# Row sums of a 64 MB tensor on one core: a two-part layout, sums of big tiles on one engine, an early main store, and loads issued ahead of the opening barrier

## The chip, the cores and the metric

The kernel runs on 1 core of one Trainium2 chip. The metric is device time in microseconds (us); lower is better. All runs named here are of state fast, and every profile shows a granted clock of 1.0. A profile covers one execution, and its span is about 1.8 us shorter than the device time of the same execution (162.6 against 164.42 for the profile of the kernel before).

Names used below: DVE is VectorE, ACT is ScalarE, POOL is GpSimd, SP is SyncE, which issues all DMAs here. "SPq" is SP's instruction sequencer. The "opening barrier" is the wait at the start of the program that holds each engine until the others are there too (in the trace SP waits for PE's sequencer). A load "lands" when all 16 counts of its semaphore have arrived in the trace.

## The reference

```python
batch, seq, dim = 32, 512, 1024
x = np.random.randn(batch, seq, dim).astype(np.float32)      # 67.1 MB
out = (np.sum(x, axis=-1) / float(dim)).astype(np.float32)   # 16,384 sums, 64 KB
```

One pass over 67.1 MB, and hardly any output. The 16,384 rows are spread over 128 partitions, so each partition has J = 128 rows of D = 1024 floats (4 KB each).

## The kernel before

Each partition owns 128 neighbouring rows, so in HBM the partitions of one load are 512 KB apart. Nine big loads (eight of 14 rows, one of 8) go through three buffers; then come loads of 4 and 2 rows, one row, and the last row in two pieces. DVE sums most rows of a tile in one reduce; ACT sums the others one at a time through its accumulator.

```python
xr = x.tensor.reshape((P, J, D)).ap()
out_v = out.tensor.reshape((P, J)).ap()
bulk = [14] * 7 + [14, 8]
split = {14: 6, 8: 4, 4: 2, 2: 1}            # rows summed on ACT
tail = [4, 2]
...
def sums(t, j, rows):
    d = rows - split[rows]
    for r in range(d, rows):
        act_sum(res[:, j + r : j + r + 1], t[:, r, :])
    nc.vector.reduce_sum(out=res[:, j : j + d], in_=t[:, :d, :], axis=AX)

for i, rows in enumerate(bulk):
    t = pool.tile([P, 14, D], F32, name="t")          # pool has 3 buffers
    tc.keep_in_program_order(nc.sync.dma_start(out=t[:, :rows, :], in_=xr[:, j : j + rows, :]))
    sums(t, j, rows)
    j += rows
...                                                   # tail tiles, one single row
c = 704
t = one.tile([P, D], F32, name="last")
tc.keep_in_program_order(nc.sync.dma_start(out=t[:, :c], in_=xr[:, j, :c]))
tc.keep_in_program_order(nc.sync.dma_start(out=t[:, c:], in_=xr[:, j, c:]))
act_sum(part[:, 2:3], t[:, :c])
nc.vector.reduce_sum(out=part[:, 3:4], in_=t[:, c:], axis=AX)
nc.vector.tensor_scalar(out=res[:, j : j + 1], in0=part[:, 3:4], scalar1=part[:, 2:3],
                        scalar2=scale, op0=ADD, op1=MULT)
tc.keep_in_program_order(nc.sync.dma_start(out=out_v, in_=res))   # one store of 64 KB
```

## Time and profile before

| | before |
|---|---|
| device time, median of 4 runs | 164.17 us (164.04 to 164.25) |
| share of the span in which the hardware DMA queue is busy, mean of 16 engines | 96.5% |
| busy DVE, ACT | 49%, 38% |
| first load issued, first tile landed | 0.73 us, 20.60 us |
| last load landed, store issued, store landed, end of span | 159.35, 160.22, 161.77, 162.65 us |

Lines of the page of the kernel before: span, busy time by engine, and the DMA queue (packets, MB, share of 16 engines' time).

```profile
span 162.6 us, 213 instructions
DVE 79.3 (49%) x16; ACT 61.1 (38%) x115; POOL 0.2 (0%) x4
q1 hardware_dynamic: 2160, 67.18, 96.5%
```

The DMA queue is the only thing that is nearly always busy. One packet of 57,344 bytes (14 rows of one partition) takes 2.116 us at the median of the trace, which is 27.1 GB/s on each of 16 engines, 434 GB/s together. 67.11 MB at that rate take 154.8 us. The rest of the span is head and tail.

Timeline of the kernel before (columns: start us, duration us, engine, line, operation, out<-in, and in brackets the idle time before it and what ended that).

```profile
0.72 1.28 ACT L50 ACT_TABLE_LOAD   x1 [0.72 <-PEq L108]
0.73 46.15 SPq L61 DMA_DIRECT2D t<-in_x_dram  x5
20.63 8.69 DVE L56 TENSOR_REDUCE res<-t 128x8 f32<-128x8192 f32 x1 [20.63 <-DMA t<-in_x_dram]
37.80 8.69 DVE L56 TENSOR_REDUCE res<-t 128x8 f32<-128x8192 f32 x1 [8.49 <-DMA t<-in_x_dram]
54.87 8.69 DVE L56 TENSOR_REDUCE res<-t 128x8 f32<-128x8192 f32 x1 [8.38 <-DMA t<-in_x_dram]
...
105.81 8.69 DVE L56 TENSOR_REDUCE res<-t 128x8 f32<-128x8192 f32 x1 [8.25 <-DMA t<-in_x_dram]
...
122.77 8.69 DVE L56 TENSOR_REDUCE res<-t 128x8 f32<-128x8192 f32 x1 [8.27 <-DMA t<-in_x_dram]
...
159.03 0.76 ACT L50 ACTIVATE junk<-last 128x704 f32<-128x704 f32 x1 [0.32 <-DMA last<-in_x_dram]
159.40 0.47 DVE L87 TENSOR_REDUCE part<-last 128x1 f32<-128x320 f32 x1
159.98 0.21 DVE L88 TENSOR_SCALAR res<-part 128x1 f32<-128x1 f32 x1
160.22 0.35 SPq L91 DMA_DIRECT2D out_dram<-res  x1
```

DVE starts the first sum 0.03 us after its tile lands and the others about as soon, so the starts of its sums tell the landings. After the first, every sum of a 14-row tile waits about 8 us for a DMA: the engines have time to spare. The first landings are 17.17 and 17.07 us apart, the later ones (105.81 to 122.77) 16.96. At the head, SP issues nothing until 0.73 us, when the opening barrier releases the engines. At the end there is a fixed sequence: last landing, two short DVE operations, store, closing barriers.

### The profile page before, as it was taken

What the parts mean: (1) busy time and instruction counts of PE and PEld (TensorE: products, weight loads), DVE (VectorE), ACT (ScalarE), POOL (GpSimd) and SP (SyncE); (2) the same over time, 40 slices, a digit from 0 to 9 for tenths busy, and PEclk for the clock granted to TensorE, in tenths of its full rate; (3) what the DMA queues carried; (4) which work ended last, traced back from release to release, by engine and by line L of the source; (5) the groups of instructions that cost most, each with busy time, mean ns of one, the idle gap of its engine ahead of it and who ended that gap; (6) DMA issues with size and microseconds to landing.
All of it is one profiled execution on the core that took longest, in us unless ns stands there. A gap on an engine that the chain in (4) does not pass through costs nothing.

```text
span 162.6 us, 213 instructions
## 1 busy us (share of the span) xinstructions
DVE 79.3 (49%) x16; ACT 61.1 (38%) x115; POOL 0.2 (0%) x4
## 2 busy tenths in 40 slices
DVE  0000099207940596039801990099108930697893
ACT  3000096006800490029201940095007700692882
POOL 0000000000000000000000000000000000000000
DMA  6999999989999999899999999999999999998990
GB/s 226 451 451 451 451 437 395 437 353 409 451 451 451 451 451 437 381 423 395 423 423 451 451 453 451 451 451 437 409 409 423 409 423 423 443 435 383 423 373 22
DMA packets 2161, 67.18 MB, mean 413 GB/s; under 512 B 240, under 2 KB 496, under 8 KB 752
## 3 DMA queue, kind: packets, MB, share of 16 engines
q1 hardware_dynamic: 2160, 67.18, 96.5%
q14 instruction: 1, 0.01, 0.0%
HBM read 67.11 MB, written 0.07 MB: 413 GB/s over the span
## 4 chain that ended last, share of the span: by engine, by line
DMA 74%; DVE 18%; another core or an unknown queue 5%; SPq 1%; issue 0%; DVEq 0%
DMA t<-in_x_dram 48%; DMA tail<-in_x_dram 25%; DVE res L56 17%; DVE part L75 0%; SPq L61 0%; SPq L66 0%; DVE part L87 0%; DVE res L79 0%; DVE res L88 0%; DVE res L76 0%; DVEq L88 0%; DVEq L76 0%; DVEq L79 0%
## 5 line engine op out<-in xcount | busy, mean ns | idle before, releaser
L56 DVE TENSOR_REDUCE res<-t 128x8 f32<-128x8192 f32 (+1 forms) x9 | 73.9, 8212 | 79.9 <-DMA t<-in_x_dram 79.9
L50 ACT ACTIVATE junk<-t 128x1024 f32<-128x1024 f32 x52 | 52.5, 1009 | 96.7 <-DMA t<-in_x_dram 96.7
L50 ACT ACTIVATION_READ_ACCUMULATOR junk<-t 128x1 f32 x52 | 9.7, 186 | 0.0
L56 DVE TENSOR_REDUCE res<-tail 128x2 f32<-128x2048 f32 (+1 forms) x2 | 3.5, 1753 | 0.7 <-DMA tail<-in_x_dram 0.7
L50 ACT ACTIVATE junk<-tail 128x1024 f32<-128x1024 f32 x3 | 3.1, 1022 | 0.9 <-DMA tail<-in_x_dram 0.9
L50 ACT ACT_TABLE_LOAD x1 | 1.3, 1283 | 0.7 <-PEq L108 0.7
L50 ACT ACTIVATE junk<-last 128x704 f32<-128x704 f32 x1 | 0.8, 761 | 0.3 <-DMA last<-in_x_dram 0.3
L75 DVE TENSOR_REDUCE part<-row 128x1 f32<-128x704 f32 x1 | 0.9, 880 | 0.0
L50 ACT ACTIVATION_READ_ACCUMULATOR junk<-tail 128x1 f32 x3 | 0.6, 186 | 0.0
L50 ACT ACTIVATE junk<-row 128x320 f32<-128x320 f32 x1 | 0.4, 441 | 0.1
L87 DVE TENSOR_REDUCE part<-last 128x1 f32<-128x320 f32 x1 | 0.5, 475 | 0.0
L79 DVE TENSOR_SCALAR res<-res 128x126 f32<-128x126 f32 x1 | 0.2, 228 | 0.1
L88 DVE TENSOR_SCALAR res<-part 128x1 f32<-128x1 f32 x1 | 0.2, 214 | 0.1
L76 DVE TENSOR_SCALAR res<-part 128x1 f32<-128x1 f32 x1 | 0.2, 214 | 0.1
L50 ACT ACTIVATION_READ_ACCUMULATOR junk<-last 128x1 f32 x1 | 0.2, 187 | 0.0
L50 ACT ACTIVATION_READ_ACCUMULATOR junk<-row 128x1 f32 x1 | 0.2, 186 | 0.0
L108 POOL MEMSET const-bfloat16-1.0<- 128x1 bf16 x1 | 0.1, 101 | 0.0
L108 POOL MEMSET const-uint8-127<- 128x1 uint8 x1 | 0.1, 101 | 0.0
L108 POOL MEMSET const-float32-0.0<- 128x1 f32 x1 | 0.1, 98 | 0.2 <-issue 0.2
L108 POOL MEMSET const-float32-1.0<- 128x1 f32 x1 | 0.1, 98 | 0.0
## 6 DMA issues: line engine op xcount, KB each, us to landing
t<-in_x_dram SPq DMA_DIRECT2D x8, 7168.0 KB, 42.1
t<-in_x_dram SPq DMA_DIRECT2D x1, 4096.0 KB, 34.8
tail<-in_x_dram SPq DMA_DIRECT2D x1, 2048.0 KB, 39.3
tail<-in_x_dram SPq DMA_DIRECT2D x1, 1024.0 KB, 41.4
row<-in_x_dram SPq DMA_DIRECT2D x1, 512.0 KB, 42.2
last<-in_x_dram SPq DMA_DIRECT2D x1, 352.0 KB, 42.6
last<-in_x_dram SPq DMA_DIRECT2D x1, 160.0 KB, 42.5
out_dram<-res SPq DMA_DIRECT2D x1, 64.0 KB, 1.5
```

The costliest lines, as they stand in the source:

```text
L50: nc.scalar.activation(junk[:, :n], src, COPY, accum_out=dst)
L56: nc.vector.reduce_sum(out=res[:, j : j + d], in_=t[:, :d, :], axis=AX)
L75: nc.vector.reduce_sum(out=part[:, 1:2], in_=t[:, :c], axis=AX)
L76: nc.vector.tensor_scalar(out=res[:, j : j + 1], in0=part[:, 1:2], scalar1=part[:, 0:1], scalar2=scale, op0=ADD, op1=MULT)
L79: nc.vector.tensor_scalar_mul(out=res[:, :j], in0=res[:, :j], scalar1=scale)
L87: nc.vector.reduce_sum(out=part[:, 3:4], in_=t[:, c:], axis=AX)
L88: nc.vector.tensor_scalar(out=res[:, j : j + 1], in0=part[:, 3:4], scalar1=part[:, 2:3], scalar2=scale, op0=ADD, op1=MULT)
L108: nc = _bacc.Bacc("TRN2", target_bir_lowering=False, num_devices=1)
```

## The change

The intent is to shorten head and tail. The first loads are moved ahead of the opening barrier; the main part of the result (120 of 128 columns) is stored while the last loads still run, so only 4 KB are left for the end; to make each store contiguous in HBM the rows are dealt out in two parts (120 rows per partition, then 8), which puts the partitions of the main part 480 KB apart instead of 512 KB; the first six big tiles are summed on DVE alone; the last row comes in three pieces. The diff cut to its core (the body of the helper and the loops are as described; `q` takes the sums of the last eight rows, `r` ACT's share of the seventh of them):

```diff
+def start_loads_at_once(nc):
+    # moves SP's first DMA copies that wait for nothing (three loads) in front of
+    # SP's drain in the first block, that is, ahead of the opening barrier
+    ...
+    nc.at_finalize(start_loads_at_once)
-    xr = x.tensor.reshape((P, J, D)).ap()
-    out_v = out.tensor.reshape((P, J)).ap()
+    L = 8
+    M = J - L
+    x_main = bass.AP(tensor=x.tensor, offset=0, ap=[[M * D, P], [D, M], [1, D]])
+    x_last = bass.AP(tensor=x.tensor, offset=P * M * D, ap=[[L * D, P], [D, L], [1, D]])
+    o_main = bass.AP(tensor=out.tensor, offset=0, ap=[[M, P], [1, M]])
+    o_last = bass.AP(tensor=out.tensor, offset=P * M, ap=[[L, P], [1, L]])
-    bulk = [14] * 7 + [14, 8]
-    split = {14: 6, 8: 4, 4: 2, 2: 1}
-    tail = [4, 2]
+    main = [(14, 0)] * 6 + [(14, 4), (14, 6), (8, 4)]      # (rows, of these on ACT)
+    last = [(4, 2), (2, 1)]
 ...
-    (last row: 704 columns on ACT, 320 on DVE, one tensor_scalar, one store of 64 KB)
+    a, b = 448, 704
+    load(pa, x_last[:, L - 1, :a])
+    load(pb, x_last[:, L - 1, a:b])
+    load(pc[:, : D - b], x_last[:, L - 1, b:])
+    nc.gpsimd.tensor_scalar_mul(out=res, in0=res, scalar1=scale)
+    tc.keep_in_program_order(nc.sync.dma_start(out=o_main, in_=res))      # behind the loads
+    act_sum(pc[:, D - b : D - b + 1], pa)
+    nc.vector.reduce_sum(out=pc[:, D - b + 1 :], in_=pb, axis=AX)
+    nc.vector.reduce_sum(out=q[:, L - 1 :], in_=pc, axis=AX)
+    nc.vector.scalar_tensor_tensor(out=fin, in0=q, scalar=scale, in1=r, op0=MULT, op1=ADD)
+    tc.keep_in_program_order(nc.sync.dma_start(out=o_last, in_=fin))
```

More of the change, by code (lines that the diff above doesn't have):

```diff
@@ L12 @@
 AX = mybir.AxisListType.X
+def start_loads_at_once(nc):
+    sp = mybir.EngineType.SP
+    first, body = nc.main_func.blocks[0], nc.main_func.blocks[1]
+    loads = []
+    for i in body.instructions:
+        if i.engine == sp:
+            if type(i).__name__ != "InstDMACopy" or (i.sync_info and i.sync_info.on_wait):
+                break
+            loads.append(i)
+    names = {i.name for i in loads}
+    assert names
+    body.instructions = [i for i in body.instructions if i.name not in names]
+    at = next(
+        k for k, i in enumerate(first.instructions) if i.engine == sp and type(i).__name__ == "InstDrain"
+    )
+    first.instructions = first.instructions[:at] + loads + first.instructions[at:]
 @with_exitstack
@@ L29 @@
     assert J * P == N
-    xr = x.tensor.reshape((P, J, D)).ap()
-    out_v = out.tensor.reshape((P, J)).ap()
-    bulk = [14] * 7 + [14, 8]
-    split = {14: 6, 8: 4, 4: 2, 2: 1}
-    tail = [4, 2]
-    assert sum(bulk) + sum(tail) + 2 == J
-    pool = ctx.enter_context(tc.tile_pool(name="bulk", bufs=3))
+    L = 8
+    M = J - L
+    x_main = bass.AP(tensor=x.tensor, offset=0, ap=[[M * D, P], [D, M], [1, D]])
+    x_last = bass.AP(tensor=x.tensor, offset=P * M * D, ap=[[L * D, P], [D, L], [1, D]])
@@ L41 @@
+    o_main = bass.AP(tensor=out.tensor, offset=0, ap=[[M, P], [1, M]])
+    o_last = bass.AP(tensor=out.tensor, offset=P * M, ap=[[L, P], [1, L]])
+    main = [(14, 0)] * 6 + [(14, 4), (14, 6), (8, 4)]
+    last = [(4, 2), (2, 1)]
+    assert sum(n for n, _ in main) == M and sum(n for n, _ in last) == L - 2
+    bulk = ctx.enter_context(tc.tile_pool(name="bulk", bufs=3))
     one = ctx.enter_context(tc.tile_pool(name="one", bufs=1))
     psum = ctx.enter_context(tc.tile_pool(name="junk", bufs=4, space=bass.MemoryType.PSUM))
-    res = one.tile([P, J], F32, name="res")
@@ L45, with load, act_sum @@
-    part = one.tile([P, 4], F32, name="part")
-    def act_sum(dst, src):
+    res = one.tile([P, M], F32, name="res")
+    fin = one.tile([P, L], F32, name="fin")
+    q = one.tile([P, L], F32, name="q")
+    r = one.tile([P, L], F32, name="r")
+    nc.gpsimd.memset(r, 0.0)
+    def load(dst, src):
+        tc.keep_in_program_order(nc.sync.dma_start(out=dst, in_=src))
+    def act_sum(dst, src, by=1.0):
         n = src.shape[-1]
         junk = psum.tile([P, D], F32, name="junk")
-        nc.scalar.activation(junk[:, :n], src, COPY, accum_out=dst)
@@ L52, in sums @@
-    def sums(t, j, rows):
-        d = rows - split[rows]
-        for r in range(d, rows):
-            act_sum(res[:, j + r : j + r + 1], t[:, r, :])
-        nc.vector.reduce_sum(out=res[:, j : j + d], in_=t[:, :d, :], axis=AX)
+        nc.scalar.activation(junk[:, :n], src, COPY, scale=by, accum_out=dst)
+    def sums(dst, t, rows, on_act):
+        d = rows - on_act
+        for i in range(d, rows):
+            act_sum(dst[:, i : i + 1], t[:, i, :])
+        nc.vector.reduce_sum(out=dst[:, :d], in_=t[:, :d, :], axis=AX)
@@ L58 @@
     j = 0
-    for i, rows in enumerate(bulk):
-        t = pool.tile([P, 14, D], F32, name="t")
-        tc.keep_in_program_order(nc.sync.dma_start(out=t[:, :rows, :], in_=xr[:, j : j + rows, :]))
-        sums(t, j, rows)
+    for rows, on_act in main:
+        t = bulk.tile([P, 14, D], F32, name="t")
+        load(t[:, :rows, :], x_main[:, j : j + rows, :])
+        sums(res[:, j : j + rows], t, rows, on_act)
         j += rows
-    for i, rows in enumerate(tail):
-        t = one.tile([P, rows, D], F32, name=f"tail{i}")
-        tc.keep_in_program_order(nc.sync.dma_start(out=t, in_=xr[:, j : j + rows, :]))
-        sums(t, j, rows)
-        j += rows
@@ L71 @@
-    c = 704
-    t = one.tile([P, D], F32, name="row")
-    tc.keep_in_program_order(nc.sync.dma_start(out=t, in_=xr[:, j, :]))
-    act_sum(part[:, 0:1], t[:, c:])
-    nc.vector.reduce_sum(out=part[:, 1:2], in_=t[:, :c], axis=AX)
-    nc.vector.tensor_scalar(
-        out=res[:, j : j + 1], in0=part[:, 1:2], scalar1=part[:, 0:1], scalar2=scale, op0=ADD, op1=MULT
-    )
-    nc.vector.tensor_scalar_mul(out=res[:, :j], in0=res[:, :j], scalar1=scale)
-    j += 1
-    t = one.tile([P, D], F32, name="last")
@@ L84 @@
-    tc.keep_in_program_order(nc.sync.dma_start(out=t[:, :c], in_=xr[:, j, :c]))
-    tc.keep_in_program_order(nc.sync.dma_start(out=t[:, c:], in_=xr[:, j, c:]))
-    act_sum(part[:, 2:3], t[:, :c])
-    nc.vector.reduce_sum(out=part[:, 3:4], in_=t[:, c:], axis=AX)
-    nc.vector.tensor_scalar(
-        out=res[:, j : j + 1], in0=part[:, 3:4], scalar1=part[:, 2:3], scalar2=scale, op0=ADD, op1=MULT
-    )
-    tc.keep_in_program_order(nc.sync.dma_start(out=out_v, in_=res))
+    j = 0
+    for rows, on_act in last:
+        t = one.tile([P, rows, D], F32, name=f"t{rows}")
+        load(t, x_last[:, j : j + rows, :])
+        sums(q[:, j : j + rows], t, rows, on_act)
+        j += rows
@@ new lines @@
+    c = 768
+    row = one.tile([P, D], F32, name="row")
+    load(row, x_last[:, j, :])
+    act_sum(r[:, j : j + 1], row[:, c:], by=scale)
+    nc.vector.reduce_sum(out=q[:, j : j + 1], in_=row[:, :c], axis=AX)
+    a, b = 448, 704
+    pa = one.tile([P, a], F32, name="pa")
+    pb = one.tile([P, b - a], F32, name="pb")
+    pc = one.tile([P, D - b + 2], F32, name="pc")
+    load(pa, x_last[:, L - 1, :a])
+    load(pb, x_last[:, L - 1, a:b])
+    load(pc[:, : D - b], x_last[:, L - 1, b:])
+    nc.gpsimd.tensor_scalar_mul(out=res, in0=res, scalar1=scale)
```

## The prediction

> **What bounds it now.** The load stream. By the page's queue part the hardware DMA queue is busy 96.5% of 16 engines' span, while DVE is busy 49% and ACT 38%. In the trace's packets, one of 57,344 bytes takes 2.116 us at the median: 27.1 GB/s on each of 16 engines, 434 GB/s together; 67.11 MB at that rate is 154.8 of the 162.6 us. In the timeline the 14-row tiles land 16.9 to 17.2 us apart. This is at the 435 GB/s ceiling that the Trainium skill gives ("DMA: Bandwidth & Descriptors", section Bandwidth); nothing in the change raises it.
>
> So only what lies outside the stream can move the time:
> - Head (queue's timeline): first load issued at 0.73 us, after the opening barrier; first packet at 1.74; the first packets are slow (2.5 to 3.0 us), about 0.6 us in all.
> - Tail: the last load lands at 159.35; DVE ends at 160.19, the store is issued at 160.22, its first packet starts at 161.07, it lands at 161.77, and the closing barriers end at 162.65.
>
> **What the change does.**
> 1. Loads ahead of the barrier: first issue from 0.73 to about 0.0. All 0.7 us is on the critical path. SP reaches the barrier after three issues (about 1.3 us), so ACT and DVE start later; they wait until 20 us for data, so that is free.
> 2. Big tiles on DVE alone: 8 rows take 8.69 us and 4 rows 4.42, so 1.07 us a row, about 15.1 us for 14, under the 17 us between landings. The buffer returns 15 us after landing instead of 8.7, with two loads queued behind it (about 19 us of work), so the stream doesn't starve. Nothing gained or lost: off the critical path.
> 3. Layout, 120 and 8 rows: the same bytes in the same large packets; the pitch between partitions becomes 480 KB instead of 512. The packets before show only some 0.75 us of slowness over the middle (mostly from 25 to 70 us), so this is worth between -0.5 and +0.3; I take -0.05. A third piece of the last row: eight more small packets per engine, +0.1 us with its landing.
> 4. Main store queued behind the loads: 61 KB leave the end; the scaling moves to POOL, done about 5 us before the end. The last store is 4 KB (32 bytes per partition). Only the 0.35 us of packet time shrinks, by perhaps 0.15; issue to first packet (0.85 us) and receipt (0.35 us) stay.
> 5. Last row: ACT does 448 columns, DVE 256, then DVE must reduce 322 after both, then multiply-add. From the last landing: the 256-column reduce ends 0.06 us after it, +0.12 wait, +0.48 reduce, +0.11 wait, +0.21: issue about 1.0 us after landing instead of 0.87, so +0.14.
>
> **Sum.** -0.73 (barrier) +0.1 (third piece) -0.05 (layout) +0.14 (DVE tail) -0.15 (store) = about -0.7 us. Predicted 163.55 us; 8 times in 10 between 163.0 and 164.2. Faster by over 2%: 1%; within 2%: 98%; slower by over 2%: 1%.
>
> **What would show it.** Queue's timeline: first issue near 0, first packet near 1.0, first tile landing near 19.9. Landings still 16.9 to 17.1 apart. DVE's 14-row sums near 15.1 us, idle about 1.9 us before each. The end: last landing near 158.7, final store issued about 1.0 us later and landing 1.3 to 1.5 us after that.
>
> **What would make it wrong.** The new pitch changing the packet time; the 32-byte writes landing slowly; the main store's packets colliding with the last loads or the last store; the device time not counting the 0.7 us of barrier; or DVE's 14-row sums taking over 17 us, which would starve the queue.

## The result, and the profile after

| | before | after |
|---|---|---|
| device time, median of 4 runs | 164.17 us (164.04 to 164.25) | 162.98 us (162.87 to 163.29) |

The ratio is 0.9931, 95% interval 0.9914 to 0.9948. The gain is 1.2 us by the medians where 0.7 was forecast. It is within 2%, as predicted, but the median lies 0.02 us below the low end of the stated range.

Page of the kernel after, the same lines as before:

```profile
span 161.5 us, 138 instructions
DVE 120.0 (74%) x15; ACT 20.7 (13%) x39; POOL 0.8 (0%) x6
q1 hardware_dynamic: 2448, 67.18, 97.1%
```

DVE took over ACT's work, and the queue is as busy as it was. Timeline of the kernel after:

```profile
0.00 52.27 SPq L76 DMA_DIRECT2D t<-in_x_dram  x5
1.73 1.28 ACT L81 ACT_TABLE_LOAD   x1 [1.73 <-PEq L144]
19.92 15.09 DVE L87 TENSOR_REDUCE res<-t 128x14 f32<-128x14336 f32 x1 [19.92 <-DMA t<-in_x_dram]
36.83 15.09 DVE L87 TENSOR_REDUCE res<-t 128x14 f32<-128x14336 f32 x1 [1.82 <-DMA t<-in_x_dram]
53.78 15.09 DVE L87 TENSOR_REDUCE res<-t 128x14 f32<-128x14336 f32 x1 [1.86 <-DMA t<-in_x_dram]
...
157.58 0.55 ACT L81 ACTIVATE junk<-pa 128x448 f32<-128x448 f32 x1
157.87 0.42 DVE L124 TENSOR_REDUCE pc<-pb 128x1 f32<-128x256 f32 x1
158.07 0.18 ACT L81 ACTIVATION_READ_ACCUMULATOR junk<-pa 128x1 f32 x1
158.38 0.49 DVE L125 TENSOR_REDUCE q<-pc 128x1 f32<-128x322 f32 x1
158.98 0.17 DVE L126 SCALAR_TENSOR_TENSOR fin<-q,r 128x8 f32<-128x8 f32 x1
159.17 0.34 SPq L127 DMA_DIRECT2D out_dram<-fin  x1
```

The first load is issued at 0.00 instead of 0.73. ACT's table load, released by the same barrier, starts 1.0 us later than before, and nothing waits for it. The first landings are 16.91 and 16.95 us apart, not 17.17 and 17.07. The last load lands at 158.25, so the store is issued 0.92 us after it, where the kernel before needed 0.88.

DMA issues of the two stores after, and of the one store before (KB each, us from issue to landing):

```profile
out_dram<-res SPq DMA_DIRECT2D x1, 60.0 KB, 5.1
out_dram<-fin SPq DMA_DIRECT2D x1, 4.0 KB, 1.4
```

```profile
out_dram<-res SPq DMA_DIRECT2D x1, 64.0 KB, 1.5
```

The main store is queued behind the last loads and lands 5.1 us after its issue; the small one lands 0.14 us sooner after its issue than the big one did (1.41 against 1.55 in the trace).

It helps to cut each span at three points: the first issue, the first landing, and the eighth landing (the last tile of 14 rows).

| stretch, us | before | after | difference |
|---|---|---|---|
| start of span to first issue | 0.73 | 0.00 | -0.73 |
| first issue to first landing | 19.87 | 19.90 | +0.03 |
| first to eighth landing | 119.07 | 118.58 | -0.49 |
| eighth landing to end of span | 22.97 | 23.04 | +0.07 |

The 0.73 was predicted, and so was the near zero of the last line. The 0.49 in the middle of the load stream was not. These are two single executions, however, and the profile of the kernel before fell on the slowest of its runs up to then (164.42).

### The profile page after: what moved, and what is told of

It reads as the page before. It is cut to its first block, busy times and chain, and to the rows that moved or that the text cites. A ratio compares the mean times of both kernels' runs of the same rounds, so it can differ in the third digit from the quotient of the medians.

```text
span 161.5 us, 138 instructions
## 1 busy us (share of the span) xinstructions
DVE 120.0 (74%) x15; ACT 20.7 (13%) x39; POOL 0.8 (0%) x6
## 4 chain that ended last, share of the span: by engine, by line
DMA 67%; DVE 29%; another core or an unknown queue 1%; SPq 1%; issue 0%; DVEq 0%
DMA t<-in_x_dram 45%; DVE res L87 28%; DMA row<-in_x_dram 22%; SPq L76 1%; DVE q L107 1%; DVE q L125 0%; DVE pc L124 0%; DVE fin L126 0%; DVEq L125 0%; DVEq L126 0%
## 5 line engine op out<-in xcount | busy, mean ns | idle before, releaser
L87 DVE TENSOR_REDUCE res<-t 128x14 f32<-128x14336 f32 (+3 forms) x9 | 114.4, 12716 | 38.2 <-DMA t<-in_x_dram 38.2
L81 ACT ACTIVATE junk<-t 128x1024 f32<-128x1024 f32 x17 | 17.2, 1013 | 135.6 <-DMA t<-in_x_dram 135.6
L87 DVE TENSOR_REDUCE q<-t 128x2 f32<-128x2048 f32 (+1 forms) x2 | 3.5, 1752 | 0.7 <-DMA t<-in_x_dram 0.7
L81 ACT ACTIVATION_READ_ACCUMULATOR junk<-t 128x1 f32 x17 | 3.2, 188 | 0.0
L120 POOL TENSOR_SCALAR res<-res 128x120 f32<-128x120 f32 x1 | 0.5, 513 | 151.0 <-DVE res L87 151.0
L107 DVE TENSOR_REDUCE q<-row 128x1 f32<-128x768 f32 x1 | 1.0, 953 | 0.1
L125 DVE TENSOR_REDUCE q<-pc 128x1 f32<-128x322 f32 x1 | 0.5, 489 | 0.1
L81 ACT ACTIVATE junk<-pa 128x448 f32<-128x448 f32 x1 | 0.5, 547 | 0.1
```

Of the source, the lines that this page charges most:

```text
L81: nc.scalar.activation(junk[:, :n], src, COPY, scale=by, accum_out=dst)
L87: nc.vector.reduce_sum(out=dst[:, :d], in_=t[:, :d, :], axis=AX)
L107: nc.vector.reduce_sum(out=q[:, j : j + 1], in_=row[:, :c], axis=AX)
L120: nc.gpsimd.tensor_scalar_mul(out=res, in0=res, scalar1=scale)
L125: nc.vector.reduce_sum(out=q[:, L - 1 :], in_=pc, axis=AX)
```

## The experiments

Kernels whose names start with b_ are the kernel before with one thing altered; those with a_ are the kernel after with one thing altered. Theory A: the middle got faster because of the load addresses (512 KB between partitions became 480). Theory B: it got faster because the engines use the buffers differently. Theory C: it is chance of single executions, and worth nothing on average.

### b_again: the kernel before, unchanged

> The kernel before, unchanged: a control for noise and a second trace of its middle. Both theories expect 164.17 us (ratio 1.000 within 0.001). In the first trace the eighth 14-row tile landed 119.07 us after the first, and the landings of tiles 2 to 4 were 17.18, 17.07 and 17.10 us apart against 16.91 to 16.95 later. Theory A (the address pattern, partitions 512 KB apart) expects the slow stretch again: 119.0 to 119.2 us. A third theory, chance of one execution, expects 118.6 to 119.3 us, with the slow stretch elsewhere or absent.

164.13 us (ratio 1.000, 0.9988 to 1.0012). The second trace has no slow stretch: 118.61 us from the first to the eighth landing. Load rate in the first three intervals between landings, first trace (columns: stretch, length, busy time of DVE, ACT, POOL, clock, DMA share, GB/s):

```profile
20.00:37.00 17.00, 8.69 (x1) 6.34 (x12) 0.00 (x0) 1.00 1.00 425
37.00:54.00 17.00, 8.69 (x1) 6.35 (x12) 0.00 (x0) 1.00 0.98 418
54.00:71.00 17.00, 8.69 (x1) 6.34 (x12) 0.00 (x0) 1.00 1.00 432
```

The same stretches of the second trace, b_again:

```profile
20.00:37.00 17.00, 8.69 (x1) 6.35 (x12) 0.00 (x0) 1.00 1.00 432
37.00:54.00 17.00, 8.69 (x1) 6.34 (x12) 0.00 (x0) 1.00 1.00 432
54.00:71.00 17.00, 8.69 (x1) 6.34 (x12) 0.00 (x0) 1.00 1.01 439
```

The same kernel with the same engine work moved 425 and 418 GB/s in one execution and 432 in the other. So the slow stretch comes and goes: the 0.49 us of the first comparison is not a fixed property, and Theory A in its strict form ("always") is wrong. The span of the second trace is 162.26 us, which is nearer to the usual run.

### b_barrier: only the loads moved ahead of the barrier

```diff
+    nc.at_finalize(start_loads_at_once)      # with the helper, nothing else
```

> The kernel before with only the loads moved ahead of the opening barrier. Both theories expect 0.7 us less than before (163.45 us, ratio 0.9957): first issue at 0.0, first tile landing at 19.9, and the middle (first to eighth landing) still 119.0 to 119.2 us. If the barrier alone were worth all that the change gained, it would be 162.98.

163.53 us, ratio 0.9963 (0.9951 to 0.9975): 0.6 us faster. The first issue is at 0.00 and the first landing at 19.83; the middle is 119.06 us. The head is as expected, and the time lies 0.1 us above the expected 163.45, which is within the noise. The barrier alone does not explain the whole gain.

### b_layout: only the load addresses

```diff
-in_=xr[:, j : j + rows, :]
+in_=x_main[:, j : j + rows, :]               # 480 KB apart; x_last for the last 8 rows
```

> The kernel before with only the load addresses changed: 120 rows per partition, 8 in a second part. The sums go to the old places, so the result is wrong on purpose (right sums, in a different order). Theory A (the middle of the stream was slow because of the address pattern) expects 118.6 us from the first to the eighth landing and 163.7 us in all (ratio 0.997). Theory B (the middle was slow because ACT and DVE both read the buffers during the loads, or because buffers return at another moment) expects no change: 119.07 us and 164.17.

163.86 us, ratio 0.9987 (0.9976 to 0.9999): 0.2 us faster, just clear of noise. Its output is wrong, which doesn't matter for the time. The middle took 118.69 us and the first landing came 19.73 us after the first issue.

### b_dve: only the split between DVE and ACT

```diff
-        d = rows - split[rows]
+        d = rows - (4 if j == 84 else 0 if rows == 14 and j < 84 else split[rows])
```

> The kernel before with only the split changed: tiles 1 to 6 on DVE alone, tile 7 with 4 rows on ACT, the rest as before. Theory A (address pattern) expects no change: 119.07 us from the first to the eighth landing, 164.17 us in all. Theory B (ACT's reads or the moment of the buffer's return slow the loads) expects 118.6 us and 163.7. DVE's 14-row sums 15.1 us in both.

164.20 us, ratio 1.0004 (0.9991 to 1.0017): nothing. Its trace shows a slow stretch again (118.97 us) although ACT is idle there. Theory B falls: ACT's reads are not what makes it.

### a_again: the changed kernel, unchanged

> The changed kernel, unchanged: a control and a second trace. The first batch showed that the slow stretch of the middle comes and goes between executions of the kernel before (119.07 and 118.61 us from first to eighth landing). Theory A' (the parts add up: barrier -0.7, layout -0.2, end of the kernel -0.05 to -0.1, average over executions) expects 163.0 to 163.2 us. Theory C (the gain of the first comparison held a lucky 0.4 us in the middle) expects 163.3 to 163.5.

162.97 us, ratio 0.9925 (0.9910 to 0.9940). The gain is confirmed at 1.2 us; Theory C (163.3 to 163.5) is wrong, and the time is just below the range of Theory A' (163.0 to 163.2). In this trace the middle is 118.59 us, no shorter than b_again's 118.61, yet its span is 161.07 against 162.26. Of these 1.19 us, 0.73 is the issue, 0.02 the middle, and 0.51 the stretch from first issue to first landing (19.44 us against 19.95), less 0.06 that the end takes longer. So there is a second place where the new kernel can gain: the first tile.

### a_pitch512: the changed kernel with the old addresses

```diff
-x_main = bass.AP(tensor=x.tensor, offset=0, ap=[[M * D, P], [D, M], [1, D]])
-x_last = bass.AP(tensor=x.tensor, offset=P * M * D, ap=[[L * D, P], [D, L], [1, D]])
+x_main = bass.AP(tensor=x.tensor, offset=0, ap=[[J * D, P], [D, M], [1, D]])
+x_last = bass.AP(tensor=x.tensor, offset=M * D, ap=[[J * D, P], [D, L], [1, D]])
 # and the stores likewise, so the result is right
```

> The changed kernel with the old addresses, partitions 512 KB apart in both parts (result right, stores strided). Theory A' (the layout matters on average, by rarer slow packets or a better start) expects +0.2 to +0.3 us over the changed kernel run in the same rounds. Theory C (the layout is worth nothing, the 0.2 us of the first batch was noise) expects 0.0, within 0.1.

163.58 us, ratio 0.9957 (0.9938 to 0.9977) against 0.9925 (0.9910 to 0.9940) for a_again in the same rounds: 0.5 us slower by the ratios, 0.6 by the medians, and more than either theory expected. The intervals just touch, but all six runs (163.12 to 163.83) lie above all five of a_again (162.85 to 163.07). It gives back over 40% of the gain of the whole change by addresses alone; order and kind of all instructions are those of the changed kernel. (The addresses of the stores change too; a_p512_onestore below, which stores as the kernel before does, is no faster than this one clear of noise.) The two traces differ by 0.40 us up to the first landing, 0.22 in the middle and 0.11 at the end. In the head one can see where the difference begins. These are windows of the first microseconds (a packet is counted where it starts, so 1835 GB/s over 0.5 us is 16 packets of 57,344 bytes, one on each engine). The kernel after:

```profile
1.00:1.50 0.50, 0.00 (x0) 0.00 (x0) 0.00 (x0) 1.00 6.06 1835
1.50:2.00 0.50, 0.00 (x0) 0.27 (x1) 0.10 (x1) 1.00 0.00 0
2.00:2.50 0.50, 0.00 (x0) 0.50 (x1) 0.00 (x0) 1.00 0.00 0
```

The same windows of a_pitch512:

```profile
1.00:1.50 0.50, 0.00 (x0) 0.00 (x0) 0.00 (x0) 1.00 3.47 1147
1.50:2.00 0.50, 0.00 (x0) 0.26 (x1) 0.10 (x1) 1.00 1.34 459
2.00:2.50 0.50, 0.00 (x0) 0.50 (x1) 0.00 (x0) 1.00 0.65 229
```

In the first of these traces (480 KB) all 16 engines start within half a microsecond. With 512 KB 10 start, then 4, then 2: the last one starts 2.02 us after the first issue.

But the packets that start together also take longer. The DMA share in these lines is the packets' own time over the window, as a share of 16 engines, so the 16 first packets take 3.03 us each on average with 480 KB (6.06 times 0.5) and 2.73 with 512 KB. In these two traces the last of them ends 4.77 and 4.69 us after the first issue, and the first tile lands after 19.90 and 19.84: in this execution the earlier start bought nothing. Over all 14 traces the first landing comes 15.10 to 15.19 us after the last of the 16 first packets has ended (by the packets of the trace; seven more of 2.116 us, 14.8 in all, follow on each engine). So what counts for the head is that end, and not the start of the sixteenth engine.

### a_act: the changed kernel with the old split

```diff
-    main = [(14, 0)] * 6 + [(14, 4), (14, 6), (8, 4)]
+    main = [(14, 6)] * 8 + [(8, 4)]
```

> The changed kernel with the old split, 6 of 14 rows on ACT in each big tile. Both theories expect no change against the changed kernel (within 0.1 us): the sums are off the critical path either way. A rival in which ACT's reads slow the loads expects +0.3 or more, with packets over 2.116 us spread over the middle.

163.11 us, ratio 0.9938 against 0.9925: 0.2 us slower than a_again, more than expected, but inside the intervals (0.9922 to 0.9954 and 0.9910 to 0.9940). Its trace has one landing interval of 17.11 us and is otherwise like a_again's. b_dve moved the other way (DVE alone was 0.07 us slower by its ratio). The two together show no effect of the split that is clear of noise; one of up to about 0.2 us is not excluded.

### a_p512_onestore: one store at the end

```diff
-    res = one.tile([P, M], F32, name="res")
-    fin = one.tile([P, L], F32, name="fin")
+    whole = one.tile([P, J], F32, name="whole")
+    res, fin = whole[:, :M], whole[:, M:]
-    ...dma_start(out=o_main, in_=res)
-    ...dma_start(out=o_last, in_=fin)
+    ...dma_start(out=out.tensor.reshape((P, J)).ap(), in_=whole)
```

> The changed kernel with the old addresses and one store of 64 KB at the very end, instead of 60 KB queued behind the loads and 4 KB at the end. To be compared with a_pitch512, which differs in the store alone. If the early store is worth what its landing times say (1.55 us from issue to landing before, 1.41 after), +0.15 us over a_pitch512, with 1.55 us again in the trace. If it is worth nothing, 0.0; if the receipts of 512-byte rows also delay the closing barrier, +0.3 or more.

The diff is cut, and against a_pitch512.

163.38 us, ratio 0.9953 (0.9938 to 0.9969) against 0.9957 for a_pitch512: no slower, where +0.15 was one of the three expectations. The intervals are too wide to exclude +0.15 by times alone. The trace does show 1.54 us from issue to landing instead of 1.41. But without the main store in the queue the last load landed 19.73 us after the eighth instead of 19.88, and the closing took 0.83 us after the store's landing instead of 0.93. From the eighth landing to the end it is 23.09 us against 23.14. With the early store the last store lands 0.13 us sooner after its issue, but the last load lands 0.15 later; 0.09 of that is hidden, because DVE was still busy with the middle piece (the store is issued 1.00 us after the last landing without it, 0.91 with it). The 0.10 at the close is the order in which SP waits for its semaphores (see a_oldtail below). Net, no gain of the early store shows.

### a_pitch508 and a_contig: other distances between partitions

```diff
# a_pitch508
-x_main = bass.AP(tensor=x.tensor, offset=0, ap=[[M * D, P], [D, M], [1, D]])
+x_main = bass.AP(tensor=x.tensor, offset=0, ap=[[127 * D, P], [D, M], [1, D]])
# a_contig: each tile one contiguous stretch, partitions 56 KB apart
-        load(t[:, :rows, :], x_main[:, j : j + rows, :])
+        part = bass.AP(tensor=x.tensor, offset=P * j * D, ap=[[rows * D, P], [D, rows], [1, D]])
+        load(t[:, :rows, :], part)
```

> The changed kernel, main part's partitions 508 KB apart instead of 480 (wrong result on purpose: 7 of 127 rows are skipped per partition). So far, with partitions 512 KB apart, the sixteenth queue's first packet started 2.0 us or more after the first issue and the first tile landed 19.83 to 19.98 us after it (six traces); with 480 KB, 1.35 to 1.6 us and 19.44 to 19.90 us (four traces). If it is the power of two that hurts, 508 KB behaves like 480: 1.6 us or less, 163.0 us. If it is closeness to 512 KB or the mere size of the pitch, it behaves like 512: 2.0 us, 163.5.

> The changed kernel, each tile of the main part one contiguous stretch of memory, partitions 56 KB apart (wrong result on purpose: right sums in another order). If the power of two is what hurts, this is like 480 KB: 163.0 us, within 0.15. If any smaller pitch is better, the start gets better still: under 1.35 us to the sixteenth queue's first packet and under 162.9 us in all.

Their outputs are wrong, which doesn't matter for the times. a_pitch508: 163.08 us, ratio 0.9930 (0.9914 to 0.9946); the sixteenth engine starts 1.36 us after the issue. a_contig: 163.03 us, ratio 0.9925 (0.9909 to 0.9940); 1.43 us. So 508 KB behaves like 480 KB and like 56 KB: being 4 KB off 512 is enough, and a smaller distance brings no more.

### a_oldtail: an attempt at a version that beats both

```diff
-    (last row in three pieces: 448 on ACT, 256 on DVE, 320 + 2 partial sums on DVE)
+    load(end[:, :704], x_last[:, L - 1, :704])
+    load(end[:, 704:], x_last[:, L - 1, 704:])
+    act_sum(part[:, 2:3], end[:, :704])
+    nc.vector.reduce_sum(out=part[:, 3:4], in_=end[:, 704:], axis=AX)
+    nc.vector.tensor_scalar(out=fin[:, L - 1 :], in0=part[:, 3:4], scalar1=part[:, 2:3],
+                            scalar2=scale, op0=ADD, op1=MULT)
```

> An attempt at a version that beats both: the changed kernel with the last row cut as in the kernel before (two pieces, 704 columns on ACT and 320 on DVE). From the eighth landing to the end the kernel before took 22.98 us and the changed one 23.03 to 23.05. If the third piece costs what the landings say, the last load lands 0.06 us earlier against the eighth (19.71), the store is issued 0.88 us after it instead of 0.92, and the stretch takes 22.9 us: about 0.1 us less than the changed kernel, 162.9 us.

The cut leaves out that the row before the last is also split as in the kernel before (704 columns on DVE), and that the first six of the last eight sums are scaled early.

162.77 us (162.68 to 162.88), ratio 0.9908 (0.9890 to 0.9926), result correct. It was not run in the same rounds as the changed kernel, and the intervals of the two ratios overlap (0.9925 for a_again), so by times alone "faster than the changed kernel" is likely but not proved. The trace gives the reason: from the eighth landing to the end 22.84 us against 23.03 to 23.04. The end of its timeline:

```profile
157.63 0.76 ACT L79 ACTIVATE junk<-last 128x704 f32<-128x704 f32 x1 [0.35 <-DMA last<-in_x_dram]
158.02 0.49 DVE L119 TENSOR_REDUCE part<-last 128x1 f32<-128x320 f32 x1
158.61 0.21 DVE L120 TENSOR_SCALAR fin<-part 128x1 f32<-128x1 f32 x1
158.85 0.34 SPq L123 DMA_DIRECT2D out_dram<-fin  x1
```

Its DVE starts the last reduce 0.03 us after the landing (157.99); in the changed kernel that reduce has to wait for the reduce of the middle piece and starts 0.13 us after it. The other part is at the close. SP waits there for the semaphores one after the other; in the changed kernel the one of the last store is third of five, with two more behind it (0.93 us from landing to end), in a_oldtail it is the last (0.83 us). The same holds for the kernel before, with one wait behind it (0.88), and for a_p512_onestore, with none (0.83).

### a_nobarrier: the changed kernel with its loads behind the barrier

```diff
-    nc.at_finalize(start_loads_at_once)
```

> The changed kernel with its loads back behind the opening barrier. The parts taken one by one from the kernel before gave -0.59 us (barrier) and -0.20 (layout), together -0.79, against -1.22 for the whole change; taken away from the changed kernel, the layout was worth 0.54. If the parts only add up and the differences are noise of single batches, this is 0.6 to 0.75 us slower than the changed kernel: about 0.50 to 0.62 us faster than the kernel before in the same rounds. If the early start and the layout help each other, it is about 0.95 us slower than the changed kernel: only 0.2 to 0.3 us faster than the kernel before, with the first tile landing 19.7 us or more after the first issue.

163.71 us, ratio 0.9974 (0.9960 to 0.9987): 0.43 us faster than the kernel before, which lies between the two expectations (0.50 to 0.62, and 0.2 to 0.3). The interval, about 0.2 to 0.65 us, holds both, so the times don't decide between them. The first tile landed 19.62 us after the first issue, where the second expectation wanted 19.7 or more. Against a_again's ratio the early issue is worth 0.8 us here, and 0.6 in b_barrier; the traces say 0.73. With the 0.73 of the traces the parts add up: 0.43 + 0.73 = 1.16. That the early start and the layout help each other is neither shown nor excluded.

### All traces together

| kernel | distance of partitions | first issue to 16th engine's first packet, us | first issue to first landing | first to eighth landing | eighth landing to end |
|---|---|---|---|---|---|
| before | 512 KB | 2.01 | 19.87 | 119.07 | 22.97 |
| b_again | 512 KB | 1.97 | 19.95 | 118.61 | 22.97 |
| b_barrier | 512 KB | 2.00 | 19.83 | 119.06 | 22.97 |
| b_dve | 512 KB | 2.25 | 19.98 | 118.97 | 22.98 |
| a_pitch512 | 512 KB | 2.02 | 19.84 | 118.81 | 23.14 |
| a_p512_onestore | 512 KB | 1.98 | 19.88 | 118.58 | 23.09 |
| b_layout | 480 KB | 1.51 | 19.73 | 118.69 | 22.97 |
| after | 480 KB | 1.48 | 19.90 | 118.58 | 23.04 |
| a_again | 480 KB | 1.59 | 19.44 | 118.59 | 23.03 |
| a_act | 480 KB | 1.35 | 19.49 | 118.75 | 23.01 |
| a_oldtail | 480 KB | 1.57 | 19.70 | 118.56 | 22.84 |
| a_nobarrier | 480 KB | 1.56 | 19.62 | 118.61 | 23.02 |
| a_pitch508 | 508 KB | 1.36 | 19.57 | 118.59 | 23.04 |
| a_contig | 56 KB | 1.43 | 19.51 | 118.58 | 23.06 |

With 512 KB, whatever else the kernel does, the sixteenth engine starts 1.97 to 2.25 us after the issue, else after 1.35 to 1.59. The last of the 16 first packets ends 4.68 to 4.83 us after the issue with 512 KB, else 4.34 to 4.77 (the 4.77 is the trace "after"): about half of the earlier start is used up by longer first packets. The mean of the first landing is 19.89 against 19.62, and of the middle 118.85 against 118.62: 0.27 + 0.23 = 0.5 us. In the middle four of six traces with 512 KB are at 118.8 or more, and none of the other eight. The last column hardly moves; only a_oldtail is clearly lower.

## Why the prediction was right or wrong

- **What bounds it: right.** The queue stays at 97%, and packets of 57,344 bytes take 2.116 us at the median before and after. Everything gained is outside the steady stream or in its disturbances.
- **Loads ahead of the barrier, -0.73: right.** First issue 0.00, first packet 1.00 us later as before. In device time 0.6 us (b_barrier) and 0.8 us (a_nobarrier). The barrier's delay for the other engines cost nothing, as said.
- **Big tiles on DVE alone, 0: right.** 15.09 us per tile and 1.8 us idle, forecast 15.1 and 1.9; b_dve and a_act show no effect beyond noise.
- **Layout, "I take -0.05": wrong, and the reason why the total was missed.** The prediction saw the slow packets of 25 to 70 us and the possible -0.5, but put its middle value next to zero. The runs show -0.2 us when the layout is added to the kernel before and 0.5 us lost when it is taken from the changed one; the traces put it at 0.5 on average. Half of that the prediction didn't consider at all: it noted "the first packets are slow", "about 0.6 us in all", as a fact of the head and did not ask whether the first packets (started from 1.74 to 2.74 us in the trace before) depend on the addresses. They do: their starts come closer together, and on average the last of them ends earlier, though not in the profiled run of the changed kernel, whose head is no shorter than before (+0.03).
- **End of the kernel, +0.1 (third piece) +0.14 (DVE) -0.15 (store) = +0.09: right in sum, in part by luck**, measured +0.06 to +0.07 from the eighth landing to the end. In its parts: the last load came 0.10 us later against the eighth (19.77 to 19.78 instead of 19.67), the DVE tail cost 0.05 rather than 0.14, the store saved 0.14, and the close took 0.05 us longer, which was not foreseen (one more wait of SP behind the store's). The 0.10 is not the third piece alone: without the early store it is 0.06 (a_p512_onestore, 19.73), and with the early store but two pieces 0.07 (a_oldtail, 19.74). "The main store's packets colliding with the last loads" was named as a risk; a_p512_onestore shows that the early store gains nothing net.

**How far this is shown.** That 512 KB costs time and 480, 508 and 56 KB do not, with the same instructions otherwise, is shown by times and traces. Why it does is not shown: no run here looks behind the packets, and the earlier start of the sixteenth engine goes with the gain without explaining its size. Why the slow stretches appear in some executions alone is open, and so is how much of the 0.23 us of the middle comes from which executions happened to be profiled, and so is why b_layout's gain (0.2) is smaller than a_pitch512's loss (0.5); each interval is about 0.2 to 0.3 us wide to either side, so this may be noise.

## What to carry to other kernels

When a kernel is at the DMA rate, look for time only before the first packet, in how soon the last of the 16 engines is done with its first packet, and after the last landing; and issue the first loads ahead of anything they need not wait for. Try another distance where the partitions of a load are 512 KB apart: here a few KB off gave half a microsecond for free. Other powers of two were not tried. A cut into smaller last pieces, or an earlier store, has to be weighed with its own waits and landings; here the simpler last row was the better one.

## What the Trainium skill lacked or had wrong

- "DMA: Bandwidth & Descriptors", section Latency and other measured facts, row on HBM row pitch at large powers of two: it gives 207 GB/s for a pitch of 512 KiB beside 214 for a padded 4 MiB pitch, measured on copies between HBM tensors, so a steady loss that can be estimated from these two figures at about 3%. Here, for loads into SBUF, the steady packet time is the same at 512 and 480 KB (2.116 us at the median); with 512 KB the start is spread over 1 us (16th engine at 1.97 to 2.25 us instead of 1.35 to 1.59), the first tile lands later (19.89 us on average instead of 19.62) and slow stretches come in some executions, 0.5 us of 164 in all. Its advice to go a few KiB off agrees: 508 KB was as good as 480.
- Same page, section Specifications: transfers under 512 B are said to cost a read-modify-write. The last store in rows of 32 bytes (4 KB) landed 1.41 us after its issue, the store in rows of 512 bytes (64 KB) 1.55; by the packets of the traces, one of 32 bytes took 9 ns at the median and one of 512 bytes 27. No penalty shows in a store this small.
- Same page, section Bandwidth, neither lacking nor wrong: the ceiling of 435 GB/s agrees: 27.1 GB/s on each of 16 engines, 434 together.
- No page says what the opening barrier of a kernel's own program costs, or that loads may be issued ahead of it: the first issue moved from 0.73 to 0.00 us, and 0.6 to 0.8 us of device time went with it.
